# Weight splits, sums and casts moved behind copies and small steps in a two-layer hybrid trunk

## The chip, the cores and the metric

The kernel runs on one core of one Trainium2 chip. The metric is the device time of one execution in microseconds (us); the time before is the median of three runs. All arithmetic that feeds the matrix engine is in float32 split in two parts: a rounded high part (`fp32r`, names that end in H) and a low part (value minus high part, names that end in L). A product is then three matmuls: high by high, high by low, low by high.

## The reference

The model is a decoder trunk of two layers on 512 tokens of width 1024. Cut to what matters here:

```
for l in range(2):
    sh1, sc1, gt1, sh2, sc2, gt2, sh3, sc3, gt3 = c_act @ w_ada[l] + b_ada[l]
    hn = rms_norm(h, g_ffn1[l]) * (1 + sc1) + sh1
    h  = h + 0.5 * (1 + gt1) * swiglu(hn, w_ffn1_in[l], w_ffn1_out[l])     # D_FF = 2816
    hn = rms_norm(h, g_mix[l]) * (1 + sc2) + sh2
    proj = hn @ w_mix_in[l]                      # attention | RWKV-7 | short conv
    h  = h + (1 + gt2) * (concat(att, rwkv, conv) @ w_mix_out[l])
    hn = rms_norm(h, g_ffn2[l]) * (1 + sc3) + sh3
    h  = h + 0.5 * (1 + gt3) * swiglu(hn, w_ffn2_in[l], w_ffn2_out[l])
rms_norm(x, g) = x * rsqrt(mean(x * x) + 1e-6) * g
```

In the attention the queries and the keys are also RMS-normed, per head of 64.

## The kernel before

Activations lie transposed: eight tiles `h0` to `h7` of 128 features by 512 tokens stay on chip for the whole run. The six sublayers (ffn1, mix, ffn2 of layer 0, then of layer 1) run one after the other. Each weight tile (128 by 8 by 128, 512 KB) is loaded by SyncE (SP), cast to its high part by ScalarE (ACT, `split`, line 94) and its low part is made by VectorE (DVE, line 95: source minus high part). The matrix engine (PE) then runs lines 89, 90 and 91 for each block of 128. A tile framework puts the program's instructions into one queue for each engine; an engine works its queue strictly in order, so an instruction that waits holds up all that are behind it on its engine. Four buffers of each of `wH` and `wL` exist, so a cast also waits until the matmuls have done with the pair of buffers four before it.

**The ffn** (from line 288). Its first two pairs of hidden tiles (four in the very first sublayer) are made by plain matmuls. The other pairs are made by `pair_in`, in which seven products of half size take the place of eight. They are named by their accumulators: `ps_d`, `ps_f` and `ps_g`, lines 370 to 372. A sum of weights `S` is made in steps: the first two blocks are added by the DMA as they land (`plus`, GpSimd's queue), then `a11` (tile `first`) is added by VectorE (line 393) and `a12` (tile `wraw`) too (line 403), and after each step `S` is split again. ScalarE copies intermediate products out: `up` (388), `s1` (392; in profile rows the buffer is `s`), `s2` (397). The second factor, w_out, is worked in two groups of hidden tiles; the profile has eight places in all where the pairs of one group begin, in the four ffns two each.

**The end of an ffn** (from line 484). The last two tiles of the output, 6 and 7, are computed in two halves of 256 tokens. `residual` (283) adds them to `h`, `square` (199) squares them, `add_ss` (195) sums the squares in `ss`. `stats` (218 to 221) sums over features by matmuls with a column of ones (`ps_ss`), takes the root on ScalarE and the reciprocal on VectorE (`rstd`); `spread` (228) spreads it over partitions by matmuls (`ps_rstd`), and `apply` (235 to 237) makes the next sublayer's input `hnH`, `hnL` in steps of three instructions for each of the eight tiles. In the code `stats` of the first half stands in the middle of the matmuls of the second half of tile 6. There are three such ends ahead of a sublayer whose first three weight tiles are loaded early (`nxt`, line 491, into the buffers `first`, `third`, `sum1`): ffn1 to mix of layer 0, ffn2 of layer 0 to ffn1 of layer 1, and ffn1 to mix of layer 1. The next sublayer starts there with three tiles side by side, half by half (`projector`, lines 262 to 269: 3 tiles by 8 blocks by 3 matmuls for each half).

**The start of the mix** (from line 572). The three tiles are the keys, the values and the first pair of query heads. The keys are squared (585), copied (`kt`, 587), their squares summed over each head by a float32 matmul of 512 columns (`ps_ks`, 542), and `rk` (590, 591) scales `kt` (592). The later query tiles come one by one.

## Time and profile before

| what | us |
|---|---|
| median of three runs | 1939.34 |
| the three runs | 1935.11, 1939.34, 1943.50 |
| the profiled execution | 1942.88 |
| its span, first to last instruction | 1940.8 |
| PE busy | 1904.2 (98%) |
| DVE busy | 1402.3 (72%) |
| ACT busy | 837.2 (43%) |

Mean granted clock of the matrix engine in the profiled execution: 0.993 of full speed. Matmuls are pipelined, so that their durations overlap: a 128x256 matmul is listed with 0.28 us, and in an undisturbed stretch one starts each 0.12 us. A busy share of 98% thus does not say that no time is lost; the starts of successive matmuls do. In the profile's groups, "idle before, releaser" is the time in which an engine stood still just ahead of an instruction and what ended it.

### The profile page before, as it was taken

Reading aid. Unit: us, or ns where it says so; the run is one execution under the profiler, and the core shown is the slowest. Engines: PE = TensorE matmul, PEld = TensorE weight load, DVE = VectorE, ACT = ScalarE, POOL = GpSimd, SP = SyncE. Lnnn points to the kernel's source line nnn. Section 1 sums busy time; section 2 is a strip of 40 time slices with the busy share of each in tenths; the row PEclk is TensorE's granted clock in tenths of the full one; section 3 lists DMA queues with packets and bytes.
Section 4 is the critical chain, followed back from the end, with each engine's and each line's share of the span. In section 5 each row is a group of like instructions: output and inputs, shape, how many; then the busy total and the mean of one; then the engine's idle time right before and its main releaser. Section 6 shows DMA issues by size and latency. Waiting matters only on the chain.

```text
span 1940.8 us, 33354 instructions
## 1 busy us (share of the span) xinstructions
PE 1904.2 (98%) x13664; PEld 1675.8 (86%) x13664; DVE 1402.3 (72%) x2183; ACT 837.2 (43%) x1272; POOL 130.8 (7%) x212
## 2 busy tenths in 40 slices
PE   8999999999999999999989999999999999999999
PEld 6898899886777899899889989989767788988998
DVE  6687687758976877677858776776589677773862
ACT  4443255346432554155345524543563234532541
POOL 0101100000000001110100020110000000010000
PEclk8999999999999999999999999999999999999999
DMA  7657876611211475876726678662211125664741
GB/s 295 247 163 227 255 194 188 203 68 47 63 51 61 141 198 180 275 207 190 236 73 194 171 256 240 190 218 102 87 54 58 58 74 172 182 210 133 193 132 66
DMA packets 104312, 308.23 MB, mean 159 GB/s; under 512 B 23392, under 2 KB 24416, under 8 KB 103136
## 3 DMA queue, kind: packets, MB, share of 16 engines
q1 hardware_dynamic: 75936, 203.34, 30.6%
q0 software_dynamic: 28224, 102.77, 20.6%
q8 instruction: 107, 1.75, 0.4%
q14 instruction: 45, 0.37, 0.1%
HBM read 302.66 MB, written 3.41 MB: 158 GB/s over the span
## 4 chain that ended last, share of the span: by engine, by line
PE 68%; DVE 11%; DMA 10%; issue 6%; ACT 3%; POOL 1%; SPq 0%; DVEq 0%; ACTq 0%; POOLq 0%
PE ps_mm L89 10%; PE ps_mm L90 10%; PE ps_mm L91 10%; PE ps_d L370 6%; PE ps_d L371 6%; PE ps_d L372 6%; DMA wada<-in_wadaT 4%; PE ps_f L372 3%; PE ps_f L370 3%; PE ps_f L371 3%; DVE wL L95 3%; DVE wada L152 2%; PE ps_g L372 2%; ACT wH L94 1%; PE ps_g L371 1%
## 5 line engine op out<-in xcount | busy, mean ns | idle before, releaser
L94 ACT CAST wH<-wraw 128x1024 fp32r<-128x1024 f32 (+2 forms) x292 | 267.1, 922 | 518.8 <-PE ps_mm L90 243.8
L95 DVE TENSOR_TENSOR wL<-wraw,wH 128x1024 fp32r<-128x1024 f32 (+2 forms) x292 | 307.8, 1059 | 110.6 <-ACT wH L94 108.8
L89 PE MATMUL ps_mm<-actH,wH 128*128 128x512 f32 (+1 forms) x784 | 290.1, 370 | 0.0
L91 PE MATMUL ps_mm<-actH,wL 128*128 128x512 f32 (+1 forms) x784 | 289.4, 369 | 0.4 <-DVE wL L95 0.4
L90 PE MATMUL ps_mm<-actL,wH 128*128 128x512 f32 (+1 forms) x784 | 289.3, 369 | 0.0
L89 PE MATMUL ps_mm<-hnH,wH 128*128 128x512 f32 (+1 forms) x760 | 278.2, 370 | 6.8 <-ACT hnH L94 2.9
L91 PE MATMUL ps_mm<-hnH,wL 128*128 128x512 f32 (+1 forms) x760 | 276.7, 365 | 0.5 <-DVE wL L95 0.5
L90 PE MATMUL ps_mm<-hnL,wH 128*128 128x512 f32 (+1 forms) x760 | 275.3, 363 | 0.4
L370 PE MATMUL ps_d<-comH,wH 128*128 128x256 f32 x816 | 228.4, 280 | 4.7 <-ACT s L392 4.3
L371 PE MATMUL ps_d<-comL,wH 128*128 128x256 f32 x816 | 226.6, 278 | 0.0
L372 PE MATMUL ps_d<-comH,wL 128*128 128x256 f32 x816 | 226.3, 277 | 0.0
L152 DVE SCALAR_TENSOR_TENSOR wada<-wada,crep 128x1024 f32<-128x1024 f32 x140 | 167.8, 1221 | 49.8 <-DMA wada<-in_wadaT 49.5
L95 DVE TENSOR_TENSOR wL<-sum,wH 128x1024 fp32r<-128x1024 f32 x102 | 124.9, 1225 | 69.4 <-ACT wH L94 63.9
L89 PEld LDWEIGHTS ps_mm<-hnH,wH 128*128 128x128 f32 x760 | 143.9, 191 | 35.8 <-issue 6.7
L94 ACT CAST wH<-sum 128x1024 fp32r<-128x1024 f32 x102 | 107.2, 1051 | 152.5 <-PE ps_d L371 69.5
L91 PEld LDWEIGHTS ps_mm<-actH,wL 128*128 128x128 f32 x784 | 149.0, 190 | 24.9 <-DVE wL L95 0.8
L90 PEld LDWEIGHTS ps_mm<-actL,wH 128*128 128x128 f32 x784 | 149.1, 190 | 24.2
L89 PEld LDWEIGHTS ps_mm<-actH,wH 128*128 128x128 f32 x784 | 149.0, 190 | 24.3
L91 PEld LDWEIGHTS ps_mm<-hnH,wL 128*128 128x128 f32 x760 | 144.9, 191 | 24.6 <-issue 3.2
L90 PEld LDWEIGHTS ps_mm<-hnL,wH 128*128 128x128 f32 x760 | 144.8, 191 | 23.8 <-issue 2.8
L370 PEld LDWEIGHTS ps_d<-comH,wH 128*128 128x128 f32 x816 | 154.3, 189 | 7.5 <-ACT s L392 5.5
L371 PEld LDWEIGHTS ps_d<-comL,wH 128*128 128x128 f32 x816 | 154.3, 189 | 0.0
(354 smaller groups left out, 3907.3 us busy)
## 6 DMA issues: line engine op xcount, KB each, us to landing
wada<-in_wadaT POOLq DMA_DIRECT2D x128, 512.0 KB, 4.8
wraw<-in_wmi SPq DMA_DIRECT2D x40, 512.0 KB
wraw<-in_w2p SPq DMA_DIRECT2D x36, 512.0 KB
wraw<-in_w1p SPq DMA_DIRECT2D x32, 512.0 KB
wraw<-in_w1o SPq DMA_DIRECT2D x32, 384.0 KB
wraw<-in_w2o SPq DMA_DIRECT2D x32, 384.0 KB
wraw<-in_w1i SPq DMA_DIRECT2D x20, 512.0 KB
wraw<-in_w1o SPq DMA_DIRECT2D x32, 320.0 KB
```

The lines of the kernel that those rows point to most:

```text
L89: mm(acc, wH, xH, start=start, stop=False)
L90: mm(acc, wH, xL, start=False, stop=False)
L91: mm(acc, wL, xH, start=False, stop=stop)
L94: nc.scalar.copy(hi, src)
L95: nc.vector.tensor_sub(lo, src, hi.bitcast(F32))
L152: stt(w, w, 1.0, crep, ALU.mult, ALU.mult, accum_out=out_)
L370: mm(pt[:, i], wH, x[k][0], start=start and i + k == 0, stop=False, skip_group_check=True)
L371: mm(pt[:, i], wH, x[k][1], start=False, stop=False, skip_group_check=True)
L372: mm(pt[:, i], wL, x[k][0], start=False, stop=k == 3, skip_group_check=True)
```

## The change

The change has four parts; no instruction is added or removed, and no arithmetic differs.

1. **The ends of an ffn.** The early weights for the next sublayer are still loaded at the same place, but each is split later: the first behind the square and the sum of tile 6's first half, the second and third behind `rstd` of the first half. `split(..., behind=True)` puts the cast behind the latest small step on ScalarE and the low part behind the latest on VectorE. The fourth weight tile (the first that `projector` loads itself) is split behind the last `hnH` and `hnL` of the second half.
2. **The sums of weights.** `S += a11` and `S += a12` stand behind the low part of `a11` and `a12` on VectorE, where they stood ahead or beside.
3. **The last split of `S`** in a pair is cast behind the copy `s1` on ScalarE.
4. **The keys' norm** (`ps_ks`, `rk`, the scaling of `kt`) is issued after the copy of the second query tile; squares and copy of the keys stay.

```diff
--- before.py
+++ after.py
@@ -90,9 +90,16 @@
         mm(acc, wH, xL, start=False, stop=False)
         mm(acc, wL, xH, start=False, stop=stop)
 
-    def split(hi, lo, src):
-        nc.scalar.copy(hi, src)
-        nc.vector.tensor_sub(lo, src, hi.bitcast(F32))
+    latest = {}
+
+    def queue_behind(name):
+        return tc.issue_after(latest[name].ins) if name in latest else nullcontext()
+
+    def split(hi, lo, src, behind=False):
+        with queue_behind("act") if behind else nullcontext():
+            nc.scalar.copy(hi, src)
+        with queue_behind("dve") if behind else nullcontext():
+            return nc.vector.tensor_sub(lo, src, hi.bitcast(F32))
 
     ALL = slice(0, T)
     HALVES = (slice(0, T // 2), slice(T // 2, T))
@@ -192,11 +199,11 @@
             act(ss[:, sl], h[0][:, sl], AF.Square)
         else:
             sq = square(i, sl)
-            tt(ss[:, sl], ss[:, sl], sq, ALU.add)
+            latest["dve"] = tt(ss[:, sl], ss[:, sl], sq, ALU.add)
 
     def square(i, sl):
         sq = E("sq")[:, sl]
-        act(sq, h[i][:, sl], AF.Square)
+        latest["act"] = act(sq, h[i][:, sl], AF.Square)
         return sq
 
     def norm(l, g, ish, isc, ss):
@@ -217,8 +224,8 @@
                 for n, x in enumerate(parts):
                     mm(pt[:, b : b + 1], x, ones[:, :1], start=n == 0, stop=n == len(parts) - 1)
             r = E("rstd")[:, :2]
-            act(r, pt, AF.Sqrt, bias=vals["eps"], scale=1.0 / D)
-            nc.vector.reciprocal(r, r)
+            latest["act"] = act(r, pt, AF.Sqrt, bias=vals["eps"], scale=1.0 / D)
+            latest["dve"] = nc.vector.reciprocal(r, r)
             rstd[sl.start] = r
 
         def spread(sl):
@@ -233,20 +240,20 @@
                 a, b, sh = hn[i][0][:, sl], hn[i][1][:, sl], mod[l, ish][:, i : i + 1]
                 t = E("hn_t")[:, : T // 2]
                 stt(t, h[i][:, sl], gm[:, i : i + 1], rstd[sl.start], ALU.mult, ALU.mult)
-                act(a, t, AF.Identity, bias=sh)
-                stt(b, t, sh, a.bitcast(F32), ALU.add, ALU.subtract)
+                latest["act"] = act(a, t, AF.Identity, bias=sh)
+                latest["dve"] = stt(b, t, sh, a.bitcast(F32), ALU.add, ALU.subtract)
 
         return hn, scale, stats, spread, apply
 
 
     loads = []
 
-    def load_w(src, n=KD, raw=None, pair=None):
+    def load_w(src, n=KD, raw=None, pair=None, behind=False):
 
         w = raw or wp.tile([P, KD, P], F32, name="wraw", tag="wraw", bufs=2)
         wH, wL = pair or (wp.tile([P, KD, P], F32R, name=x, tag=x, bufs=4) for x in ("wH", "wL"))
         loads.append(nc.sync.dma_start(w[:, :n], src))
-        split(wH[:, :n], wL[:, :n], w[:, :n])
+        split(wH[:, :n], wL[:, :n], w[:, :n], behind)
         return wH, wL
 
     def projector(srcs, hn, tags, pts=None, ahead=0, ready=()):
@@ -255,7 +262,8 @@
         ws = list(ready)
 
         def fetch(n):
-            ws.extend(load_w(s) for s in srcs[len(ws) : n])
+
+            ws.extend(load_w(s, behind=bool(ready) and len(ws) == 3) for s in srcs[len(ws) : n])
 
         if pts is None:
             fetch(3)
@@ -309,9 +317,12 @@
                     done[0] = f()
                 waiting.clear()
 
-            def hl(w):
+            def hl(w, add_to=None):
                 pair = tuple(wp.tile([P, KD, P], F32R, name=x, tag=x, bufs=4) for x in ("wH", "wL"))
-                split(*pair, w)
+                parted = split(*pair, w)
+                if add_to is not None:
+                    with tc.issue_after(parted.ins):
+                        tt(add_to, add_to, w, ALU.add)
                 return pair
 
             def raw(src, tag=None):
@@ -387,25 +398,25 @@
                 up = half_("up")
                 nc.scalar.copy(up, pF)
                 a11 = raw(A(0, 0), "first")
-                prod(pD, hl(a11), B11, True)
+                prod(pD, hl(a11, S), B11, True)
                 s1 = half_("s1")
-                nc.scalar.copy(s1, pD)
-                tt(S, S, a11, ALU.add)
+                copied = nc.scalar.copy(s1, pD)
                 flush()
                 prod(pD, hl(S), P2, False)
                 s2 = half_("s2")
                 nc.scalar.copy(s2, pD)
                 a12 = raw(A(0, 1))
-                prod(pG, hl(a12), B21, True)
+                prod(pG, hl(a12, S), B21, True)
                 gate = half_("gate")
                 tt(gate, pG, s1, ALU.add)
                 act(gate, gate, AF.Silu)
-                tt(S, S, a12, ALU.add)
                 S3 = raw(A(0, 0), "third")
                 plus(S3, A(1, 0))
                 prod(pD, hl(S3), T3, False)
                 tt(up, pD, up, ALU.add)
-                prod(pF, hl(S), B22, False)
+                with tc.issue_after(copied.ins):
+                    last = hl(S)
+                prod(pF, last, B22, False)
                 tt(s2, pF, s2, ALU.add)
                 act(s2, s2, AF.Silu)
                 tt(up, s2, up, ALU.mult)
@@ -488,7 +499,16 @@
                 for j in (j0, j0 + n):
                     pair = tuple(ap_.tile([P, KD, P], F32R, name=x, tag="com", bufs=8) for x in ("wH", "wL"))
                     last[i, j] = load_w(w_out[l, i, :, j : j + n], n, None, pair)
-            nxt = [load_w(w, raw=ap_.tile([P, KD, P], F32, name="wraw", tag=t, bufs=1)) for w, t in zip(coming, ("first", "third", "sum1"))]
+            raws, nxt = [], []
+            for w, t in zip(coming, ("first", "third", "sum1")):
+                raws.append(ap_.tile([P, KD, P], F32, name="wraw", tag=t, bufs=1))
+                loads.append(nc.sync.dma_start(raws[-1], w))
+
+            def next_weights(n):
+                for w in raws[len(nxt) : n]:
+                    nxt.append(tuple(wp.tile([P, KD, P], F32R, name=x, tag=x, bufs=4) for x in ("wH", "wL")))
+                    split(*nxt[-1], w, True)
+
             ada_until(ap_, crep, *need)
             stats, spread, apply = then()
             sqs = []
@@ -500,11 +520,14 @@
                         if sl is HALVES[1]:
                             if (i, j) == (6, j0 + 5):
                                 stats(HALVES[0], sqs)
+                                next_weights(3)
                             elif (i, j) == (7, j0):
                                 spread(HALVES[0])
                                 apply(HALVES[0])
                     if i == 6:
                         residual(pt, i, cg, ss, sl)
+                        if sl is HALVES[0]:
+                            next_weights(1)
                     else:
                         sqs = [last_residual(pt, i, cg, ss, sl)]
             stats(HALVES[1], sqs)
@@ -585,11 +608,7 @@
             act(sq, pt, AF.Square)
             kt = A("kt")
             nc.scalar.copy(kt, pt)
-            pk = headsum(sq, "ps_ks")
-            rk = EA("rk")
-            act(rk, pk, AF.Sqrt, bias=vals["eps"], scale=1.0 / CH)
-            nc.vector.reciprocal(rk, rk)
-            stt(kt, kt, gqk, rk, ALU.mult, ALU.mult)
+            ksq = sq
             pt = yield from tile_()
             vr = EA("vr")
             nc.scalar.copy(vr, pt)
@@ -605,6 +624,12 @@
             for i in range(4):
                 pt = yield from tile_()
                 nc.scalar.copy(qr[:, i], pt)
+                if i == 1:
+                    pk = headsum(ksq, "ps_ks")
+                    rk = EA("rk")
+                    act(rk, pk, AF.Sqrt, bias=vals["eps"], scale=1.0 / CH)
+                    nc.vector.reciprocal(rk, rk)
+                    stt(kt, kt, gqk, rk, ALU.mult, ALU.mult)
                 sq = EA("qsq")
                 act(sq, pt, AF.Square)
                 yield
```

On VectorE at the end of ffn1 of layer 0 (h6, h7: the residual; ss: sum of squares; wL_3459 to wL_3471: low parts of the next sublayer's three weights, wL_3913 the fourth's) the queue was this before:

```order
L195 TENSOR_TENSOR ss_482<-ss_482,sq_3430 128x512
L95 TENSOR_TENSOR wL_3459<-wraw_3457,wH_3458 128x1024
L95 TENSOR_TENSOR wL_3465<-wraw_3463,wH_3464 128x1024
L95 TENSOR_TENSOR wL_3471<-wraw_3469,wH_3470 128x1024
L283 SCALAR_TENSOR_TENSOR h6_94<-ps_mm_3493,cg_1454,h6_94 128x256
L95 TENSOR_TENSOR wL_3913<-wraw_3911,wH_3912 128x1024
L195 TENSOR_TENSOR ss_482<-ss_482,sq_3525 128x256
L283 SCALAR_TENSOR_TENSOR h7_96<-ps_mm_3528,cg_1454,h7_96 128x256
L221 RECIPROCAL rstd_3586<-rstd_3586 128x2
L283 SCALAR_TENSOR_TENSOR h6_94<-ps_mm_3562,cg_1454,h6_94 128x256
L235 SCALAR_TENSOR_TENSOR hn_t_3612<-h0_82,gmod_3491,ps_rstd_3609 128x256
```

and this with the change:

```order
L202 TENSOR_TENSOR ss_482<-ss_482,sq_3430 128x512
L291 SCALAR_TENSOR_TENSOR h6_94<-ps_mm_3481,cg_1454,h6_94 128x256
L202 TENSOR_TENSOR ss_482<-ss_482,sq_3513 128x256
L102 TENSOR_TENSOR wL_3517<-wraw_3457,wH_3516 128x1024
L291 SCALAR_TENSOR_TENSOR h7_96<-ps_mm_3520,cg_1454,h7_96 128x256
L228 RECIPROCAL rstd_3578<-rstd_3578 128x2
L102 TENSOR_TENSOR wL_3582<-wraw_3459,wH_3581 128x1024
L102 TENSOR_TENSOR wL_3586<-wraw_3461,wH_3585 128x1024
L291 SCALAR_TENSOR_TENSOR h6_94<-ps_mm_3554,cg_1454,h6_94 128x256
L242 SCALAR_TENSOR_TENSOR hn_t_3612<-h0_82,gmod_3479,ps_rstd_3609 128x256
```

Tile 6's residual and sum have moved ahead of all four low parts; two of them now stand between the reciprocal and the first step of `apply`, and the fourth is far behind. The other two ends read alike, and ScalarE's casts moved in the same manner.

On ScalarE, where the first pair of a group begins (ffn2 of layer 0, first group: wH_6852 is the cast of the last `S`, s1 the copy), before:

```order
L388 COPY up_6721<-ps_f_6686 128x512
L94 CAST wH_6823<-third_6820 128x1024
L94 CAST wH_6852<-sum0_6690 128x1024
L392 COPY s1_6753<-ps_d_6685 128x512
L94 CAST wH_6893<-sum1_6890 128x1024
L397 COPY s2_6784<-ps_d_6685 128x512
```

and with the change:

```order
L399 COPY up_6721<-ps_f_6686 128x512
L100 CAST wH_6823<-third_6820 128x1024
L403 COPY s1_6754<-ps_d_6685 128x512
L100 CAST wH_6852<-sum0_6690 128x1024
L100 CAST wH_6893<-sum1_6890 128x1024
L407 COPY s2_6784<-ps_d_6685 128x512
```

The copy and the cast have changed places. On the matrix engine 13 matmuls of `ps_g` stood ahead of the product that reuses `ps_d` and so waits for `s1`; now 6 stand there, and the other 7 behind that product. In all eight first pairs of a group it reads like this; in the other pairs `s1` stood ahead of that cast already.

On the matrix engine at the start of the mix of layer 0 the keys' sum stood between the last of the three tiles side by side and the fourth:

```order
L89 MATMUL ps_mm_3728<-hnH_3489,wH_3470 128x256
L90 MATMUL ps_mm_3728<-hnL_3490,wH_3470 128x256
L91 MATMUL ps_mm_3728<-hnH_3489,wL_3471 128x256
L542 MATMUL ps_ks_3885<-ksq_3881,con_80 128x512
L89 MATMUL ps_mm_3917<-hnH_3475,wH_3912 128x512
```

and with the change it stands behind the whole fourth tile:

```order
L89 MATMUL ps_mm_3911<-hnH_3477,wH_3906 128x512
L90 MATMUL ps_mm_3911<-hnL_3478,wH_3906 128x512
L91 MATMUL ps_mm_3911<-hnH_3477,wL_3907 128x512
L565 MATMUL ps_ks_3937<-ksq_3881,con_80 128x512
L89 MATMUL ps_mm_3957<-hnH_3463,wH_3952 128x512
```

It has moved behind 24 matmuls of 512 columns, the values' transposes (`ps_vt`) and one tile's sums of the queries (`ps_q`). Ahead of that place the first matmul of the fourth tile waits, as before, for the copy `kt`, which frees its accumulator.

## The prediction

> **What bounds the kernel now.** I read the chain of waits first, then the waits by engine, then the matmuls one by one.
>
> ```profile
> PE 68%; DVE 11%; DMA 10%; issue 6%; ACT 3%; POOL 1%; SPq 0%; DVEq 0%; ACTq 0%; POOLq 0%
> DVE wada L152 <- DMA wada<-in_wadaT: 49.5, 36, 4.6
> L94 ACT CAST wH<-sum 128x1024 fp32r<-128x1024 f32 x102 | 107.2, 1051 | 152.5 <-PE ps_d L371 69.5
> ```
>
> Two thirds of the chain are matmuls. The change shortens none, so it can give only time in which the matmuls stand still or run at a lowered clock. The timeline of the matrix engine shows such time at the end of ffn1, layer 0 (columns: start, duration, engine and instruction, in brackets the idle time before it and what ended it):
>
> ```profile
> 377.60 0.28 PE L91 MATMUL ps_mm<-actH,wL 128*128 128x256 f32 x1
> 379.97 0.38 PE L218 MATMUL ps_ss<-ones_r,ss 128*128 128x1 f32 x2 [2.09 <-DVE ss L195]
> 380.87 0.38 PE L218 MATMUL ps_ss<-ones_r,sq 128*128 128x1 f32 x2 [0.52 <-ACT sq L199]
> 381.57 0.36 PE L89 MATMUL ps_mm<-actH,wH 128*128 128x256 f32 x1
> ```
>
> What VectorE and ScalarE did meanwhile:
>
> ```profile
> 374.56 3.50 DVE L95 TENSOR_TENSOR wL<-wraw,wH 128x1024 fp32r<-128x1024 f32 x3 [2.98 <-ACT wH L94]
> 377.97 0.48 DVE L283 SCALAR_TENSOR_TENSOR h<-ps_mm,cg,h 128x256 f32<-128x256 f32 x1
> 378.37 1.21 DVE L95 TENSOR_TENSOR wL<-wraw,wH 128x1024 fp32r<-128x1024 f32 x1
> 379.50 0.42 DVE L195 TENSOR_TENSOR ss<-ss,sq 128x256 f32<-128x256 f32 x1
> 373.48 3.91 ACT L94 CAST wH<-wraw 128x1024 fp32r<-128x1024 f32 x4 [2.62 <-DMA wraw<-in_wmi]
> 381.80 0.26 ACT L220 ACTIVATE rstd<-ps_ss,v_eps 128x2 f32<-128x2 f32 x1 [0.98 <-PE ps_ss L218]
> ```
>
> Four low parts for the next sublayer, released late by a load that lands at 373.48, stand ahead of `h6` and `ss`; the matmuls wait for those. The granted clock follows (windows; columns: busy time of PE, PEld, DVE, ACT, POOL, clock, DMA):
>
> ```profile
> 376.00:381.00 5.00, 2.39 (x19) 2.10 (x19) 4.31 (x6) 2.22 (x4) 0.00 (x0) 1.00 0.08 17
> 381.00:384.00 3.00, 3.00 (x20) 3.00 (x21) 0.27 (x2) 0.26 (x1) 0.00 (x0) 0.71 0.41 152
> 384.00:386.00 2.00, 2.00 (x13) 2.00 (x12) 0.99 (x3) 0.51 (x2) 0.00 (x0) 0.58 0.00 0
> 691.00:693.00 2.00, 1.62 (x14) 1.63 (x15) 1.10 (x1) 0.32 (x1) 0.00 (x0) 1.00 0.85 274
> 983.00:986.00 3.00, 3.00 (x16) 3.00 (x16) 0.17 (x1) 0.26 (x1) 0.00 (x0) 0.50 0.31 124
> 1334.00:1338.00 4.00, 4.00 (x22) 4.00 (x23) 0.98 (x3) 0.68 (x2) 0.00 (x0) 0.58 0.16 60
> 1645.00:1648.00 3.00, 2.85 (x13) 2.85 (x14) 0.87 (x1) 0.10 (x1) 0.00 (x0) 0.54 0.99 333
> ```
>
> **Part 1, the ends of an ffn.** The other two ends:
>
> ```profile
> 974.54 1.05 ACT L94 CAST wH<-wraw 128x1024 fp32r<-128x1024 f32 x1 [7.01 <-DMA wraw<-in_w1i]
> 977.64 0.28 PE L91 MATMUL ps_mm<-actH,wL 128*128 128x256 f32 x1
> 981.63 0.38 PE L218 MATMUL ps_ss<-ones_r,ss 128*128 128x1 f32 x2 [3.71 <-DVE ss L195]
> 983.41 0.56 PE L89 MATMUL ps_mm<-actH,wH 128*128 128x256 f32 x1
> 1331.04 0.28 PE L91 MATMUL ps_mm<-actH,wL 128*128 128x256 f32 x1
> 1332.26 0.38 PE L218 MATMUL ps_ss<-ones_r,ss 128*128 128x1 f32 x2 [0.94 <-DVE ss L195]
> 1333.16 0.38 PE L218 MATMUL ps_ss<-ones_r,sq 128*128 128x1 f32 x2 [0.52 <-ACT sq L199]
> 1333.85 0.36 PE L89 MATMUL ps_mm<-actH,wH 128*128 128x256 f32 x1
> ```
>
> A 128x256 matmul starts 0.12 us after the one before; the four `ps_ss` together take about 0.93 (380.87 to 381.57 is three of them in 0.70, and one more of 0.23). Standing still was thus 381.57 - 377.72 - 0.93 = 2.92 at the first end, 983.41 - 977.76 - 0.93 = 4.72 at the second, 1333.85 - 1331.16 - 0.93 = 1.76 at the third. The clock cost 3 x 0.29 + 2 x 0.42 = 1.71, then 3 x 0.50 = 1.50, then 4 x 0.42 = 1.68. Sum 14.3.
>
> What comes back? With the change nothing late stands ahead of `h6` and `ss`. Tile 6's first half is done 30 matmuls x 0.12 = 3.6 us before tile 7's, tile 7's 18 x 0.12 = 2.2 us before `ps_ss`; residual and square take 0.48 + 0.42. At the first end both sums wait for `ps_ss` at 377.72. The second is close: there the first weight lands 3.2 us ahead of `ps_ss` (974.54), not 4.2, its cast stands ahead of `h7`'s square, and I get 0.15 of waiting. Next late would be the two low parts between reciprocal and `apply`. From 377.72: `ps_ss` ends 378.65, root and reciprocal 0.6 later at 379.3, two casts (3.91 / 4 each) to 381.0, two low parts 1.2 behind each other to 382.4, `h6`, `hn_t`, `ss`, `hn_t`, `hnL` to 384.5. The matmuls that are left (12 of tile 6, 30 of tile 7, 5.0 us, and `ps_rstd`) end at 384.3. So the first `hnL` is 0.1 to 0.2 late at each end. I take 0.9 off for these and for the slow `ps_ss` that the second end counts twice: **gain 13.4**. If that chain were 1 us later than I put it, 3 us would go; if no wait returns, 14.3. The fourth weight, now split last, is needed only 24 x 3 x 2 matmuls (17 us) later.
>
> **Parts 2 and 3, the first pairs.** Their waits, in order of time:
>
> ```profile
> 236.80 0.39 PE L370 MATMUL ps_d<-comH,wH 128*128 128x256 f32 x1 [1.17 <-ACT s L392]
> 691.38 0.38 PE L370 MATMUL ps_d<-comH,wH 128*128 128x256 f32 x1 [1.19 <-ACT s L392]
> 835.60 0.39 PE L372 MATMUL ps_g<-hnH,wL 128*128 128x256 f32 x1 [1.21 <-DVE wL L95]
> 1045.83 0.38 PE L370 MATMUL ps_d<-comH,wH 128*128 128x256 f32 x1 [0.76 <-ACT s L392]
> 1189.00 0.39 PE L372 MATMUL ps_g<-hnH,wL 128*128 128x256 f32 x1 [0.46 <-DVE wL L95]
> 1645.15 0.55 PE L370 MATMUL ps_d<-comH,wH 128*128 128x256 f32 x1 [1.17 <-ACT s L392]
> 689.79 1.05 ACT L94 CAST wH<-sum 128x1024 fp32r<-128x1024 f32 x1 [1.32 <-DVE sum L403]
> 690.75 0.58 ACT L392 COPY s<-ps_d 128x512 f32<-128x512 f32 x1
> 828.85 1.23 DVE L393 TENSOR_TENSOR sum<-sum,first 128x1024 f32<-128x1024 f32 x1 [3.23 <-DMA first<-in_w2p]
> ```
>
> At 691 ScalarE was idle 1.32 us for the cast ahead of `s1`. The copy can start at 688.65, when `ps_d` is done, and end at 689.25 instead of 691.3; the six `ps_g` left in front end at 689.2. The 1.19 go, and with the slower first matmul behind the stop about 1.4. By the same steps 1045 gives 1.0. At 236 the copy stays held by the third load and comes only 0.95 us sooner, of which the seven matmuls moved behind (7 x 0.12 = 0.83) take most: 0.45. At 1645 the 1.17 go, and the clock's dip (3 x 0.46 = 1.4): 2.5. The beginnings near 130 and 1790 show no bracket; from their starts I get 0.3 each. Two lose: at 828.85 and in the same way at 1182 the block `first` lands late, so the sum behind its low part ends 1.2 to 1.8 us later, and the cast of `a12` stands behind the cast of that sum; the 835.60 wait grows by about 0.35, the 1189.00 one by 0.7. Together 1.4 + 1.0 + 0.45 + 2.5 + 0.6 - 1.05 = **gain 4.9**, between 2 (dip stays, losses doubled) and 7 (they don't come). In other pairs the cast of a sum waits for a buffer that matmuls free (the `wH<-sum` row above, 1.5 us idle each): the next product's weights lie ready three products (72 x 0.12 = 8.6 us) ahead, less cast and low part 2.2, so 1.2 us later costs nothing.
>
> **Part 4, the keys' norm**, from the start of the mix in layer 0:
>
> ```profile
> 408.15 0.58 ACT L587 COPY kt<-ps_mm 128x512 f32<-128x512 f32 x1
> 408.31 1.13 PE L542 MATMUL ps_ks<-ksq,con 128*128 128x512 f32 x2 [0.80 <-ACT ksq L585]
> 409.50 0.40 PE L90 MATMUL ps_mm<-hnL,wH 128*128 128x512 f32 x1
> ```
>
> The fourth tile waits for the end of `kt`, 408.73, whatever stands ahead. Before, half of `ps_ks` lay in that wait; now all of its 0.9 us is paid where matmuls stream, and the restart comes 0.4 sooner (by 408.9, not 409.3). Per mix a loss of 0.5, **1.0 in all**; from 0 to 1.8. `rk`'s reciprocal, on VectorE ahead of weights' low parts in both orders, and the later `kt` have the third to sixth query tile as cover.
>
> **Sum:** 13.4 + 4.9 - 1.0 = 17.3. The profiled execution took 1942.88, 3.5 above the median of 1939.34 and within the runs shown, so the forecast on the median's scale is 1939.3 - 17.3 = **1922**.
>
> **Rivals.**
> (a) The dips of the clock have another cause and stay at the short waits. For it: single waits of about 1.2 us, as at 691, left the clock at 1.00. Against it: every dip listed begins within 2 us of the restart. With the dips at the first and third end and at 1645 kept: 1.7 + 1.7 + 1.4 less, 1927. [...]
> (b) Loads set the pace later and swallow the gain. For it: the chain has 10% DMA, and VectorE waits 49.5 us for `wada`, up to 4.6 at a time. Against it: most loads start when matmuls free a buffer and move along. What is gained before (4.6 + 2.1 - 0.5 = 6.2) would be lost: 1928; the second end and 1045 as well (6 + 1): 1935.
> (c) The wait moves from `ss` to `apply`: the two low parts wait for casts that ScalarE gives late, 2.5 us at each end, and the clock falls again (1.6 each): 12.3 less, 1934. Against it: the times above.
> (d) Slower: the later sums hurt every pair, not two. There are 34 (three casts of `sum` each, 102). It decides if weights lie less than 1.2 us ahead of use instead of 6; each pair then pays one low part's 1.21: 41 more, 1963. Against it: the idle time in the `wH<-sum` row.
>
> **Chances.** Forecast 0.55; (a) 0.13; (b) 0.13; (c) 0.11; (d) or another loss 0.08. The likeliest's own range is 1915 to 1930; to leave out no more than 2 in 10 I reach to (b) and (c): 1912 to 1936. A measurement of this kernel tells about 0.5% (9.7 us) from no change: faster means under 1929.6. Forecast and (a) nearly all there, (b) and (c) mostly not: faster 0.69, same 0.24, slower 0.07.
>
> **What would show it.** Right: no bracket above 0.3 us before `ps_ss` in the second halves, clock 1.00 in the five microseconds behind, the three tiles side by side starting 3 to 6 us sooner; no wait for `s1` at 691 and 1045; `wL` waits at the two late loads a little longer; `ps_ks` among streaming matmuls. Wrong: a new wait for `hnL` of more than 0.5 us, dips that stay, longer waits for `first` or `wada`, or waits for `wL<-sum` in ordinary pairs.

## The result and the profile after

The changed kernel took 1921.72 us in the median of six runs (1917.97 to 1922.77); the kernel before, with three more runs beside it, 1937.64 (1933.77 to 1943.50). The ratio is 0.9911 with a 95% interval from 0.9892 to 0.9930: 0.9% faster. The forecast was 1922, a gain of 17.3; the medians give 15.9. The profiled execution took 1921.65 us, 21.2 less than that of before. That gap between the two differences matters below.

The head of the page and its chain of waits, after:

```profile
span 1919.6 us, 33361 instructions
PE 1894.1 (99%) x13664; PEld 1668.1 (87%) x13664; DVE 1402.3 (73%) x2183; ACT 835.3 (44%) x1272; POOL 130.7 (7%) x212
PE 83%; DVE 6%; DMA 6%; ACT 2%; issue 2%; POOL 0%; SPq 0%; ACTq 0%; DVEq 0%; POOLq 0%
```

VectorE's work is what it was to a tenth; of the chain that ended last, the matmuls now make 83% in place of 68%. What went is waiting.

The end of ffn1, layer 0, after: matrix engine, then VectorE, then two windows (columns as before: busy time of PE, PEld, DVE, ACT, POOL, granted clock, DMA).

```profile
374.76 0.28 PE L225 MATMUL ps_ss<-ones_r,ss 128*128 128x1 f32 x2
375.35 0.36 PE L225 MATMUL ps_ss<-ones_r,sq 128*128 128x1 f32 x2
```

```profile
376.10 0.17 DVE L228 RECIPROCAL rstd<-rstd 128x2 f32<-128x2 f32 x1 [2.12 <-ACT rstd L227]
377.04 2.36 DVE L102 TENSOR_TENSOR wL<-wraw,wH 128x1024 fp32r<-128x1024 f32 x2 [0.77 <-ACT wH L100]
379.71 0.47 DVE L242 SCALAR_TENSOR_TENSOR hn_t<-h,gmod,ps_rstd 128x256 f32<-128x256 f32 x1
381.07 0.48 DVE L244 SCALAR_TENSOR_TENSOR hnL<-hn_t,mod,hnH 128x256 fp32r<-128x256 f32 x1
```

```profile
376.00:381.00 5.00, 5.00 (x45) 5.00 (x44) 3.97 (x7) 2.79 (x5) 0.00 (x0) 1.00 0.02 3
381.00:384.00 3.00, 3.00 (x27) 2.98 (x27) 3.00 (x9) 1.98 (x4) 0.99 (x2) 1.00 0.13 44
```

No bracket stands ahead of `ps_ss` at these ends any more, the clock stays at 1.00, and 45 matmuls start in the five microseconds in which 19 did. The other two ends read the same (clock 1.00 from 968 to 978 and from 1314 to 1324). At the beginnings of the groups waits are left, and at the start of the mix (first the matrix engine, then ScalarE):

```profile
401.32 0.50 PE L89 MATMUL ps_mm<-hnH,wH 128*128 128x512 f32 x1 [1.27 <-ACT kt L610]
408.39 1.02 PE L565 MATMUL ps_ks<-ksq,con 128*128 128x512 f32 x2
826.74 0.39 PE L383 MATMUL ps_g<-hnH,wL 128*128 128x256 f32 x1 [0.73 <-DVE wL L102]
1035.22 0.39 PE L381 MATMUL ps_d<-comH,wH 128*128 128x256 f32 x1 [1.09 <-ACT s L407]
1174.80 0.39 PE L383 MATMUL ps_g<-hnH,wL 128*128 128x256 f32 x1 [1.18 <-DVE wL L102]
1624.57 0.39 PE L383 MATMUL ps_g<-hnH,wL 128*128 128x256 f32 x1 [0.71 <-DVE wL L102]
```

```profile
399.25 1.05 ACT L100 CAST wH<-wraw 128x1024 fp32r<-128x1024 f32 x1 [2.38 <-PE ps_mm L90]
400.69 0.58 ACT L610 COPY kt<-ps_mm 128x512 f32<-128x512 f32 x1
1033.64 1.05 ACT L100 CAST wH<-sum 128x1024 fp32r<-128x1024 f32 x1 [2.92 <-DMA sum<-in_w1p]
1034.59 0.58 ACT L407 COPY s<-ps_d 128x512 f32<-128x512 f32 x1
```

To say where the time went, each matmul of the products was set beside its counterpart in the first profile of before, and the lead in start time read off ahead of and behind each place. Leads in us (the first row is the yardstick):

| profile | first 50 us | ends, to behind the mix's start | first pairs, all eight | whole lead |
|---|---|---|---|---|
| before | 0 | 0 | 0 | 0 |
| before, once more | 0.9 | 3.2 | 1.7 | 6.1 |
| ends only (part 1) | 0.9 | 13.7 | -1.5 | 12.9 |
| sums only (part 2) | 1.3 | 8.3 | 2.6 | 12.5 |
| copy only (part 3) | 1.5 | 7.2 | 9.7 | 18.3 |
| changed | 0.6 | 12.7 | 8.0 | 21.3 |
| changed, again | 1.0 | 12.8 | 8.5 | 22.2 |
| changed, part 4 undone | 1.5 | 13.7 | 2.6 | 17.7 |
| parts 1 and 3 | 0.9 | 13.7 | 8.1 | 22.7 |
| two more moves | 1.2 | 15.5 | 10.5 | 27.1 |
| two more moves, again | 1.4 | 15.5 | 9.1 | 26.1 |

What is left to the whole lead, 0.3 at most either way, lies nearly all in the mixes. The two rows of before, with the same order of the queues, differ by 6.1: that is how far one profile is from another here.

### The profile page after: what moved, and what is told of

Read it like the earlier page. It is cut to its first block, busy times and chain, and to the rows that moved or that the text cites. A ratio compares the mean times of both kernels' runs of the same rounds, so it can differ in the third digit from the quotient of the medians.

```text
span 1919.6 us, 33361 instructions
## 1 busy us (share of the span) xinstructions
PE 1894.1 (99%) x13664; PEld 1668.1 (87%) x13664; DVE 1402.3 (73%) x2183; ACT 835.3 (44%) x1272; POOL 130.7 (7%) x212
## 3 DMA queue, kind: packets, MB, share of 16 engines
q8 instruction: 107, 1.75, 0.4%
HBM read 302.66 MB, written 3.41 MB: 159 GB/s over the span
## 4 chain that ended last, share of the span: by engine, by line
PE 83%; DVE 6%; DMA 6%; ACT 2%; issue 2%; POOL 0%; SPq 0%; ACTq 0%; DVEq 0%; POOLq 0%
PE ps_mm L89 14%; PE ps_mm L90 14%; PE ps_mm L91 14%; PE ps_d L381 6%; PE ps_d L383 6%; PE ps_d L382 6%; PE ps_f L381 3%; PE ps_f L383 3%; PE ps_f L382 3%; DMA wada<-in_wadaT 2%; PE ps_g L383 2%; PE ps_g L381 2%; PE ps_g L382 2%; DMA sum<-in_w1p 1%; DVE wL L102 1%
```

## The experiments

**One part at a time.** Ends only is the changed kernel with parts 2, 3 and 4 written back; copy only is the kernel before with

```diff
-                prod(pF, hl(S), B22, False)
+                with tc.issue_after(copied.ins):
+                    last = hl(S)
+                prod(pF, last, B22, False)
```

(`copied` is the copy to `s1`), sums only has `tt(S, S, a11, ...)` and `tt(S, S, a12, ...)` behind the low parts of `a11` and `a12`, and the last one of the four is the changed kernel with the five lines of the keys' norm back ahead of the values' tile.

> Only part 1 (the splits of the next sublayer's weights) on the kernel before. Theory (queues of VectorE and ScalarE held up the sums of squares; nothing later swallows what is won): the three ends come out 4.5, 6.1 and 3.4 us shorter, as in the profile of the full change, so about 14 us in all, near 1924 beside 1938; no wait above 0.3 us ahead of the sums of squares and the clock at 1.00 behind them. Rival (loads set the pace later): the steps are there, but at 236, 835, 1045, 1189 or 1645 the stalls grow and less than 8 us is left, 1930 or more.

Measured: 1924.45 us, ratio 0.9944 (0.9925 to 0.9963) to a before of 1936.58. The three ends came out as in the changed kernel to 0.03 us each; that kernel has no wait ahead of the sums of squares there and the clock at 1.00 behind them, and 0.03 us leaves no room for either. Theory confirmed; the time is 12 us shorter rather than 14. But the stalls at the beginnings stayed (the profiled execution, 1929.87 us, is the slowest of the four), and two of them show what they cost beside the wait; matrix engine and windows of this kernel:

```profile
682.03 0.39 PE L383 MATMUL ps_g<-hnH,wL 128*128 128x256 f32 x1 [0.74 <-DVE wL L102]
684.79 0.38 PE L381 MATMUL ps_d<-comH,wH 128*128 128x256 f32 x1 [1.18 <-ACT s L403]
1035.92 0.38 PE L381 MATMUL ps_d<-comH,wH 128*128 128x256 f32 x1 [1.77 <-ACT s L403]
684.00:687.00 3.00, 2.21 (x11) 2.21 (x12) 1.48 (x2) 0.73 (x2) 0.00 (x0) 0.67 0.80 251
1036.00:1039.00 3.00, 3.00 (x17) 3.00 (x18) 0.64 (x1) 0.00 (x0) 0.00 (x0) 0.60 0.82 294
```

The same 1.2 us wait left the clock at 1.00 at 691 of the first profile, where it stood alone. Here the clock fell behind it (0.67 in the window 684 to 687, 0.50 from 685.79 to 687.79), but another wait of 0.74 us stood 2.8 us ahead of it.

> Only part 3 (the last cast of the sum behind the copy s1) on the kernel before. Theory: the copy is what counts in the first pairs: the stalls at 691 and 1645 go (1.3 and 2.5 to 3.9 us with the clock's dip), the one at 236 shrinks; 5 to 8 us faster in all, around 1932. Rival (it is where loads happen to land): the wait for s1 goes but the same time returns some matmuls later as a wait for wL or for s2, under 3 us left.

Measured: 1924.66 us, ratio 0.9950 (0.9933 to 0.9968). More than the 5 to 8 us expected: the first pairs gained 9.7 over the first profile of before. No wait for `s1` is left at 236, 691 and 1645, and one of 0.24 at 1045. Neither the theory's number nor the rival: the mechanism held, its size was too small.

Its ends, whose order is the old one, are worth a look, and so are those of sums only:

> Only part 2 (both sums of weights behind the low parts) on the kernel before. Theory: the stalls for the copy s1 stay (1.2 us at 236, 691, 1645; 0.8 at 1045) and the two beginnings where the block `first` lands late lose 0.3 to 1 us each: slower by 0 to 2 us, not to be told from no change in the time. Rival: the gains at 236 and 835, which were 2.2 and 1.0 us in place of 0.45 and a loss of 0.35, come from this part: 3 us faster.

Measured: 1935.86 us, ratio 1.0006 (0.9988 to 1.0024): no change, as the theory had it, though the two places where `first` lands late (835 and 1189 of before's time) lost 1.2 and 2.3 rather than 0.3 to 1. At 236 the place led by 2.0 without a reason in the edit, as it did by 1.2 to 2.3 in every later profile.

The waits and windows at ends in copy only, then in sums only:

```profile
969.84 0.38 PE L225 MATMUL ps_ss<-ones_r,ss 128*128 128x1 f32 x2 [1.74 <-DVE ss L202]
971.00:974.00 3.00, 3.00 (x28) 3.00 (x28) 0.72 (x3) 0.56 (x2) 0.00 (x0) 1.00 0.40 153
1318.23 0.38 PE L225 MATMUL ps_ss<-ones_r,ss 128*128 128x1 f32 x2 [0.92 <-DVE ss L202]
1322.00:1324.00 2.00, 2.00 (x11) 2.00 (x10) 0.99 (x4) 0.72 (x2) 0.00 (x0) 0.50 0.00 0
```

```profile
973.39 0.38 PE L225 MATMUL ps_ss<-ones_r,ss 128*128 128x1 f32 x2 [1.15 <-DVE ss L202]
975.00:978.00 3.00, 3.00 (x28) 3.00 (x28) 1.17 (x4) 0.69 (x3) 0.00 (x0) 1.00 0.25 101
1325.07 0.38 PE L225 MATMUL ps_ss<-ones_r,ss 128*128 128x1 f32 x2 [1.60 <-DVE ss L202]
```

With the old order the second end waited 3.71 us for `ss` in the first profile, 1.74 and 1.15 here. The order sets that there is a wait; when the load lands sets how long. The first of the early casts on ScalarE starts when its load has landed; at this second end, in copy only, then sums only:

```profile
962.74 1.05 ACT L100 CAST wH<-wraw 128x1024 fp32r<-128x1024 f32 x1 [6.58 <-DMA wraw<-in_w1i]
```

```profile
966.29 1.05 ACT L100 CAST wH<-wraw 128x1024 fp32r<-128x1024 f32 x1 [7.03 <-DMA wraw<-in_w1i]
```

The last matmul ahead of `ps_ss` starts at 967.82 and at 971.96, so the casts lead it by 5.08 and 5.67. Lead and wait together are 6.82 both times, and so they are at the second and the third end of every profile with the old order there (four, with a second one of before that follows below): eight sums of 6.81 or 6.82. At the first end the sum is 6.21 to 6.22 in the three profiles that waited for `ss`, and in copy only, where the lead was 6.22, there was no such wait. So the landing of the load alone decides how long the wait is.

And a wait of 1.74 left the clock at 1.00 (971 to 974) where it read 0.50 (1322 to 1324) behind one of 0.92; the last section comes back to this.

> The changed kernel with part 4 undone (the keys' sum stands between the third and the fourth tile again). Theory: the float32 matmuls of the keys' sum are half hidden in the wait for the copy kt again, so each mix start is 0.6 us shorter than with the change: 1.2 us in all, 1920 to 1921 beside 1922, seen in the matmuls' starts rather than in the time. Rival: the wait ahead of the fourth tile grows with it and nothing is won.

Measured: 1918.79 us (1917.03 to 1925.19), ratio 0.9915 (0.9893 to 0.9936), not to be told from the changed kernel in time. In the starts the two mixes lead by 0.49 and 0.48 more than with the change: part 4 costs 1.0 in all. This kernel's lines show why, half of the sum lies in the wait:

```profile
399.75 1.12 PE L565 MATMUL ps_ks<-ksq,con 128*128 128x512 f32 x2 [0.80 <-ACT ksq L608]
1177.21 0.39 PE L383 MATMUL ps_g<-hnH,wL 128*128 128x256 f32 x1 [1.60 <-DVE wL L102]
```

The second line is a first pair with parts 2 and 3: the low part of `a12` came 1.60 us late, more than the 1.18 of the changed kernel's first profile, and the clock fell to 0.50 behind it:

```profile
1177.78:1181.19 3.41, 3.41 (x18) 3.41 (x17) 2.88 (x3) 1.05 (x1) 0.00 (x0) 0.50 0.54 154
```

This dip, and a second wait of 1.60 near 828, are most of why this row of the table has 2.6 for the first pairs, where the changed kernel has 8.0. That gave the next question.

**The parts together.** By the medians both halves of the gain measured alone are 12 us; together with the small parts they gave 15 to 17, not 23. By the ratios, to which the intervals belong, 0.9944 and 0.9950 multiply to 0.9894, or to 0.9905 with part 2's 1.0006 and the 1.0 us of part 4; the whole change stood at 0.9911 (0.9892 to 0.9930), which does not exclude that they simply add. The next kernels ask whether something is lost.

> Parts 1 and 3 without 2 and 4 (sums of weights and keys' norm stand as before). Theory now: the sums behind the low parts cost at the beginnings where a load lands late (waits of 0.4 to 1.8 us for the low part of a12 in the changed kernel), so without them the waits for wL at 682, 826, 1175 and 1625 shrink to 0.9 or less, and the whole is 1 to 4 us faster than the changed kernel: 1917 to 1920 beside 1921. If parts 1 and 3 simply added (12 us each), it would be 1913. Rival: these waits come from where the loads land in a run, and this version is as fast as the changed one.

Measured: 1919.93 us (1919.39 to 1923.17), ratio 0.9932 (0.9912 to 0.9952). The waits for `wL` at 682 and 826 were gone and the ones near 1173 and 1623 were 0.56 and 0.67. Against the changed kernel's 1921.7 that is no difference in time, and far from 1913. The before beside it took 1932.26, and the ratio lies above 0.9894: parts 1 and 3 give less together than the sum of their times alone, as far as three ratios of this spread can tell. One profile each cannot say whether part 2 costs its microsecond.

> The kernel before, written with the changed kernel's helpers but with every instruction in the old order: a second profile of it. Theory: the order of the queues is the same, so the same waits stand at the same places, but those that hang on a load's landing differ in size: at the three ends 1 to 3.5 us ahead of the sum of squares, at 236 between 0.15 and 1.3. If the order alone set them, all would come out within 0.1 us of the first profile.

Measured: 1936.75 us. Its ends and, behind two of them, the clock:

```profile
376.70 0.38 PE L225 MATMUL ps_ss<-ones_r,ss 128*128 128x1 f32 x2 [1.66 <-DVE ss L202]
972.45 0.38 PE L225 MATMUL ps_ss<-ones_r,ss 128*128 128x1 f32 x2 [0.64 <-DVE ss L202]
974.00:976.00 2.00, 2.00 (x10) 2.00 (x11) 0.17 (x1) 0.26 (x1) 0.00 (x0) 0.50 0.41 168
1327.91 0.38 PE L225 MATMUL ps_ss<-ones_r,ss 128*128 128x1 f32 x2 [1.20 <-DVE ss L202]
1329.00:1331.00 2.00, 2.00 (x10) 2.00 (x11) 0.17 (x1) 0.26 (x1) 0.00 (x0) 0.50 0.59 221
1331.00:1334.00 3.00, 3.00 (x16) 3.00 (x16) 0.48 (x1) 0.36 (x1) 0.00 (x0) 0.50 0.00 0
```

The same queues, and 1.66, 0.64 and 1.20 in place of 2.09, 3.71 and 0.94; 1.66 without a dip (the clock at 1.00 from 377.40 to 386.40), 0.64 with one. This is a likely reason why the parts seem not to add. With the old order at the ends, four profiles lost there, against ends only, 13.7, 10.5, 6.5 and 5.4 us: 9.0 in the mean. The first profile, from which the forecast was made, has the largest loss. Copy only's profile (1924.58 us, at the median of its runs) has one of the small ones, so its time held some 2.5 us that are no part of the copy. Taken by place, the parts come near the whole: 9.0 for the ends, 9.7 less 0.9 (the mean of the two profiles of before) for the first pairs, 1.0 off for part 4, in all 16.8 beside 15.9 and 16.6 measured. That is an estimate from one profile a kernel.

**The chain behind the reciprocal.** The first weight's split was moved as well:

```diff
-                        if sl is HALVES[0]:
-                            next_weights(1)
```

> The changed kernel with the first weight's split, too, moved behind the reciprocal: three low parts instead of two between it and the first step of apply. Theory (that chain ends just as the matmuls need its first hnL): one more cast and low part put it 1.0 to 1.2 us later, and the matmuls wait about 1 us at each of the three ends; 3 us slower. Rival: the chain has slack, and nothing changes at the ends.

Measured: 1922.33 us in one run. The three ends lost 1.1 us each against the changed kernel, as the theory said. The wait shows at the second half's `ss`, which stands in the same queue between two steps of `apply`; here the first of three alike:

```profile
381.13 0.38 PE L225 MATMUL ps_ss<-ones_r,ss 128*128 128x1 f32 x2 [0.74 <-DVE ss L202]
```

So two low parts fit behind the reciprocal, and a third costs 1.1 us an end.

**Two more moves.** Two waits of the changed kernel have a copy queued behind a cast that waits for something else: `kt` behind the fifth weight's cast (399.25 above, held until matmuls free a buffer), `s2` behind the next pair's first cast (1033.64 above, held by a load). Both were turned round, with part 2 undone (`behind="kt"` puts the fifth weight's cast behind `latest["kt"]`, the first queries' squares):

```diff
-            sq = EA("ksq")
-            act(sq, pt, AF.Square)
             kt = A("kt")
             nc.scalar.copy(kt, pt)
-            ksq = sq
+            ksq = EA("ksq")
+            act(ksq, kt, AF.Square)
...
-                act(sq, pt, AF.Square)
+                squared = act(sq, pt, AF.Square)
+                if i == 0:
+                    latest["kt"] = squared
...
-            ws.extend(load_w(s, behind=bool(ready) and len(ws) == 3) for s in srcs[len(ws) : n])
+            ws.extend(load_w(s, behind="kt" if len(ws) == 4 and tags == ("mm",) else bool(ready) and len(ws) == 3) for s in srcs[len(ws) : n])
...
-                prod(pF, hl(S), P1, True)
+                with tc.issue_after(copied2[0].ins) if copied2[0] else nullcontext():
+                    opening = hl(S)
+                prod(pF, opening, P1, True)
...
-                nc.scalar.copy(s2, pD)
+                copied2[0] = nc.scalar.copy(s2, pD)
```

> Parts 1, 3 and 4, the sums as before, and two further moves: the copy s2 ahead of the next pair's first cast, and at the start of the mix the copy kt (and the squares, made from it) ahead of the cast of the fifth weight. Theory: the waits for s2 (1.25 us at 1035 and 0.18 at most of the eight beginnings) and the waits for kt (1.4 us at each mix start) go, 4 us less than with parts 1 and 3 alone: 1912 to 1916. Rival: the cast that now stands later is late itself, and its matmuls wait instead: no better than parts 1 and 3.

Measured: 1917.31 us (1914.45 to 1920.26), ratio 0.9918 (0.9894 to 0.9941). To compare it with the changed kernel directly, both ran side by side:

> The changed kernel itself, beside the version with two more moves on the same chip. Theory: 1920 to 1923, and a second profile in which the three ends start as early as in the first (4.5, 6.1 and 3.4 us ahead of the first profile of before), since nothing there waits for a load any more, while the waits at the beginnings of the groups differ by a microsecond or two.

> Parts 1, 3 and 4 with the copies s2 and kt ahead of the casts, once more. Theory: the mix starts give 2 x 2.3 us less the longer keys' sum (1.6 instead of a loss of 0.2 to 0.6 each in the last profiles), the s2 waits 1 us: 3 to 6 us faster than the changed kernel on the same chip, 1916 to 1919. Rival: both equal within 2 us, since the time saved at these places comes back as waits for loads.

Measured: the changed kernel 1920.43 us (1918.62 to 1920.98), ratio 0.9914 (0.9893 to 0.9936); with two more moves 1916.50 (1914.11 to 1916.81), ratio 0.9893 (0.9868 to 0.9918). The ranges do not overlap: 3.9 us faster, inside the theory's 3 to 6, the fastest version here. The table gives 2.7 of it to the mix starts, where part 2 has no instruction; how the rest divides between the move of `s2` and the undoing of part 2 no run tells. This kernel's lines at the first of them, matrix engine and ScalarE:

```profile
398.78 0.28 PE L91 MATMUL ps_mm<-hnH,wL 128*128 128x256 f32 x1
399.02 0.50 PE L89 MATMUL ps_mm<-hnH,wH 128*128 128x512 f32 x1
398.38 0.59 ACT L612 COPY kt<-ps_mm 128x512 f32<-128x512 f32 x1 [2.49 <-PE ps_mm L91]
```

The copy starts while matmuls still run, and the fourth tile follows without a wait (1.27 us in the changed kernel). The waits for `s2` are gone in both profiles; the matmuls still waited up to 1.20 for the low part of `a12`, near 1171.

**Stops of chosen length.** To see which stop lowers the clock, spare squares of tile 7's first half were put ahead of the real one:

```diff
-                        sqs = [last_residual(pt, i, cg, ss, sl)]
+                        if sl is HALVES[0] and coming:
+                            residual(pt, i, cg, None, sl)
+                            spare = E("spare")
+                            for _ in range((6, 9, 12)[ends[0]]):
+                                act(spare[:, sl], h[i][:, sl], AF.Square)
+                            ends[0] += 1
+                            sqs = [square(i, sl)]
+                        else:
+                            sqs = [last_residual(pt, i, cg, ss, sl)]
```

> The changed kernel with 6, 9 and 12 spare squares of tile 7 on ScalarE ahead of the real one at the three ends, 0.34 us each, so that the matmuls stand still once for about 1.7, 2.1 and 3.1 us. Theory: the clock falls to 0.50 for one stretch of some 3.4 us or not at all, the more often the longer the stop; the middle lengths may go either way. [...]

> The same with 12, 9 and 6 spare squares: stops of about 3.8, 2.1 and 1.0 us. Theory: the first lowers the clock for certain, the last does not, the middle may. Rival: the middle one behaves as in the other run, because the length of the stop decides.

Measured: 1919.11 and 1923.62 us, one run each, and the stops did not come about. The tile framework queued the real square behind the first spare one, so `ps_ss` came on time and the spare work only crowded the later steps (0.4 to 0.6 us an end). Neither theory nor rival was put to the test; the clock stayed at 1.00 where nothing stopped (375.5 to 384.5, 969.5 to 978.5 and 1316.5 to 1325.5, in both).

## Why the prediction was right, point by point

The total was right to 1 us. Its parts were not all right, and two errors nearly cancelled, which was luck.

*The bound.* Right: only time in which matmuls stood or ran slow was to be had, and the busy time of VectorE did not move.

*Part 1, 13.4.* Right against the profile it was worked out from: ends only leads by 13.7 there. The chain of `ps_ss`, root, two casts, two low parts and `hnL` was just in time as worked out, and one low part more cost 1.1 us. What failed is the last step, where the sum of one profile's stalls (the execution of 1942.88 us) is taken off the median of 1939.34 as it stands. The stops at the ends depend on when a load lands, and in the first profile they were the longest of four. Over four profiles the ends were worth 9.0.

*The clock, 4.9 of the 14.3.* The dips went, so rival (a) fell. But they were not there in every run: behind the twelve old-order ends of four profiles, six dips (three in the first profile of before, two in the second, one in copy only, none in sums only). Three of three was the first profile's luck. No run shows what that rival's sum takes for granted, that the second end's dip would go and the other three stay: at the ends a stop of 1.76 us was followed by a dip, and one of 2.56 us was not. Two of the prices are short, too: the dips at 983 and 1645 run on past the ends of the windows read, for 3.41 us each, and cost 1.7, not 1.5 and 1.4.

*Parts 2 and 3, 4.9.* Undersized; the changed kernel led by 8.0 and 8.5 there (6.3 and 6.8 over the second profile of before). Four steps failed. At 236 the gain was put at 0.45 because the third load held the copy; that late load was a chance of the one profile, and the place came 1.2 to 2.3 us sooner in every later one, with the old order too. At 691 a gain of 1.4 was forecast, and it came as 1.3 in one profile; in the other the place lost 0.8, where `s2` stood behind a cast that a load held up (the changed kernel, again):

```profile
687.50 1.04 ACT L100 CAST wH<-sum 128x1024 fp32r<-128x1024 f32 x1 [3.42 <-DMA sum<-in_w2p]
689.08 0.39 PE L381 MATMUL ps_d<-comH,wH 128*128 128x256 f32 x1 [1.45 <-ACT s L407]
```

At 835 a loss of 0.35 was forecast and 1.0 and 1.6 were gained, since `first` landed earlier. At 1045 a gain of 1.0 was forecast: -0.3 in one profile and 1.1 in the other, for the same reason. That is rival (b) at two places, in a queue rather than in bandwidth. Turning the two round took this wait away, but at 1045 the low part of `a12` was late instead (leads of -0.2 and -0.6). At 1645 the gain of 3.9 and 3.7 was above the 2.5: the dip was worth 1.7, and the waits of 1.03 at 1642.40 and 0.29 at 1651.60, which the sum left out, shrank as well. That part 2 on its own wins nothing was right; whether it costs in the changed kernel stays open, with 8.0, 8.5 and 2.6 in three profiles beside 8.1 without it.

*Part 4, a loss of 1.0.* Measured 0.97.

*The rivals.* (b) in its large form did not come: with ends only the gain of the ends was still there in the time, 12 us. (c) did not come; a wait of its kind, though of 1.1 us an end and without a dip, was one low part away. (d) did not come: between 250 and 370 or 1660 and 1770, where ordinary pairs run, leads move by less than 0.05 us.

## What to carry to other kernels

A queue that works in order should have the short step that others wait for ahead of the long one that waits for a load: here that was worth 0.9%, and looking for the same pattern again (a copy behind a held cast), with part 2 undone, gave another 0.2%. Before a stall that ends in a load's landing is entered in a sum, look at a second profile of the same kernel: here one wait was 3.71 us in one profile and 0.64 in another, and the slowest execution of the four had the largest. A change that takes such waits off the path may also narrow the times: 1929.2 to 1946.2 in ten runs of before, 1918.0 to 1922.8 in twelve of the changed kernel.

## What the runs showed of the hardware

In these profiles the granted clock read 0.50 in every window that lies wholly inside a dip, and the time spent there is one stretch of 3.4 us, so that 1.7 us are lost (4 us at 0.58 behind 1334 of before: 4 x 0.42 / 0.50 = 3.4; 3 us at 0.71 and 2 at 0.58 behind 381: also 3.4) or, behind 1327.91 above, about two of them (0.50 from 1328.80 to 1335.64). The four dips of the first profile of before that lie behind its first 60 us, from start to end:

```profile
382.28:385.69 3.41, 3.41 (x18) 3.41 (x18) 0.79 (x2) 0.42 (x1) 0.00 (x0) 0.50 0.04 14
983.03:986.44 3.41, 3.41 (x17) 3.41 (x18) 0.24 (x2) 0.26 (x1) 0.00 (x0) 0.50 0.26 105
1334.60:1338.01 3.41, 3.41 (x18) 3.41 (x17) 0.83 (x2) 0.42 (x1) 0.00 (x0) 0.50 0.04 14
1645.21:1648.62 3.41, 3.41 (x16) 3.41 (x17) 0.66 (x1) 0.00 (x0) 0.00 (x0) 0.50 1.00 351
```

From one start to the next it is 600.75, 351.57 and 310.61 us: 176, 103 and 91 times 3.413, to 0.06 us. The starts of these four thus lie on a raster of such stretches. Two dips each of two more profiles agree. Their starts follow from the window of 1 us that holds both clocks (0.63 from 684.79 is 0.26 us at 1.00 and the rest at 0.50): 685.05 and 1036.62 in ends only, 351.57 apart, 103 times 3.413; 973.82 and 1328.80 in before once more, 354.98 apart, 104 times.

Which stop sets a dip off is not a matter of its length alone. With the 0.52 for the square added, stops of 0.82 and 2.56 us (copy only), 1.16, 1.97 and 2.42 (sums only) and 2.48 (before once more) at the ends left the clock at 1.00; behind 1.46 and 2.02 (before once more), 1.73 (copy only) and 1.76, 2.91 and 4.53 (before) it read 0.50. (These are the starts' excess over an undisturbed stream, less what the lowered clock itself added.) At the ends the two kinds differ in the part of a stop that falls into one stretch of the raster. Counted from 0.12 us after the start of the last product's matmul to the start of the next one, with `ps_ss` in it, the largest part in one stretch, with the raster laid through the dips of each of three profiles, was 1.75 and 1.83 (copy only) and 1.81 us (before once more) at the three ends without a dip and 2.07 to 3.41 at the six with one. In copy only the standstill of 3.49 us at 968 was cut by the raster into 1.66 and 1.83, and the clock read 1.00 behind it; the shorter one of 2.67 at 1317 had 2.07 in one stretch, and the clock fell to 0.50. At 684 of ends only the wait of 1.18 and 0.4 of the one of 0.74 lay in one stretch. That this part decides is an estimate from those nine ends and was not shown: in the kernel with part 4 undone two waits of 1.60 us, as listed, each lay wholly in one stretch, and the clock read 0.50 behind the one at 1177.21 and 1.00 behind the one at 827.88. The stops of chosen length, which were to tell, did not come about.
